# Attention probabilities of four head pairs turned by DMA transposes, in a two-layer hybrid attention trunk

## The chip, the cores and the metric

The kernel runs on one core of a Trainium2 chip. The metric is device time in microseconds (us) of one execution, the median of several runs. One execution was also recorded by the hardware profiler; all rows of the profile come from that one.

The engines of a core have the names of the profile: PE is TensorE (matrix products, with PEld its weight loads), DVE is VectorE, ACT is ScalarE, POOL is GpSimd, SP is SyncE, which does nothing here but issue transfers. Each engine works through its own queue in order. Transfers (DMAs) are issued from a queue of SP, ACT or POOL and run on 16 DMA engines that all queues share. SBUF is the on-chip memory, PSUM the accumulators of TensorE.

## The reference

There are two layers (DEPTH = 2), with 256 tokens of width 2048, all in float32. In each layer two groups of eight heads read the same stream: group A is attention over 64 keys per query that an indexer selects, group B is causal latent attention. Then come an output projection, a layer norm, a SwiGLU feed-forward of width 5632, and another layer norm.

```python
def _hybrid_mixer(x, positions, w_in, g_cq, g_ckv, w_uq, w_ukv, w_o):
    proj = jnp.einsum('bsd,de->bse', x, w_in)
    qa, ka, va, qi, wi, ki, cq, ckv, kr = jnp.split(proj, offsets, axis=-1)
    qa = _rope(...); ka = _rope(...); qi = _rope(...); ki = _rope(...)
    out_a = _dsa_attention(qa, ka, va, qi, ki, wi)
    ...
    out_b = _causal_attention(q_mla, k_mla, v_b, (MLA_NOPE + MLA_ROPE) ** -0.5)
    return jnp.einsum('bse,ed->bsd', jnp.concatenate([out_a, out_b], axis=-1), w_o)

# both attentions, per head
p = jax.nn.softmax(jnp.where(valid, logits, -jnp.inf), axis=-1)
out = jnp.einsum('...', p, v)
```

`_rope` turns the first channels of each head by an angle that depends on the position: `x1*cos - x2*sin` and `x2*cos + x1*sin`.

## The kernel before

**Weights and units.** Weights stream from HBM in units of 128 x 1024 float32 (512 KB). SP issues the load of each into one of four raw buffers (`load_raw`, L342). ACT writes its rounded upper part `wh` (L429), DVE the rest `wl` (L430); five pairs of such buffers exist (`UNITS`). TensorE then runs three products per tile of tokens and slice of the inner dimension: activations' high part by `wh` and by `wl`, and their low part by `wh` (L393 to L395). A unit is 12 such matmuls of 512 columns. A raw buffer is free again when the split has read it, a split buffer when TensorE has.

**Ticks.** Everything that is not a weight product runs as generators (`spawn`, `tick`, `step`, L297 on). After each unit `tick()` is called, and a generator that has said `yield n` goes on n units later. So the order in which the program is traced interleaves one piece of attention with each unit of weights. A scheduler then sets the order of each engine's queue at compile time from that order and its own estimate of when operands are ready; at run time every queue is followed in order. `tc.issue_after(latest["high"])` places an ACT instruction behind the newest `wh`.

**Order of one layer's attention part.** Projection blocks QI0, TA, QI1, TB, KA0 (each 8 units) and the query part of group B; `mla_half(0)`; QA0, VA0; `mla_half(1)`; KA1, QA1, VA1; then `w_o` in 24 units. There are eight pairs of heads per layer. Pairs 0 and 1 of group B run during QA0 and VA0; pairs 0 and 1 of group A (`dsa_attend`) from `mla_half(1)` on; pairs 2 and 3 of group B (`mla_attend`) during QA1; pairs 2 and 3 of group A during `w_o`. Beside them `presums` has POOL load, and DVE add up, weights for the feed-forward.

**One pair** (`attend`, L565). Logits of two heads come into PSUM; DVE scales and masks them into `lg`, one buffer for each tile of 128 queries (128 x 2 x 128 and 128 x 2 x 256, since the first tile sees only 128 keys). `softmax_head` makes probabilities. Some units later TensorE turns them, three 128x128 transposes per head (L583, recorded at L426), ACT copies the three out of PSUM into `pr` (L585), and after another unit TensorE multiplies: V's first block by 256 columns (L592), V's second block by 128 (L593). The profile counts two instructions for each float32 matmul. The result goes to `oT` in two parts.

**Head blocks** (`heads_T`, L608). A finished block of q or k goes through `rope`: DVE writes the two products `ra` and `rb` and adds them into `hd`. With `soon`, TensorE turns the result. Without it (QA0, KA1 and QA1) a DMA transpose does: ACT separates the upper and the lower 16-bit halves of each float32 word into `pl` (L630), ACT's queue issues a transpose of 16-bit elements back into `hd` (L633), and `LAND` = 5 units later ACT puts the halves together (L639). `hidden_by_dma` does the same for the feed-forward, issued by SP (L1074). `dup_rope` (L644) treats the small shared rows in the same way as `heads_T` does.

**Small buffers.** `t2` hands out 2 KB buffers: four that last for the whole kernel and six more during the attention part. All of `lg`, `pr`, `hd`, `ra`, `rb`, `pl`, `dup` and `rel` come from there, in turn by a count.

Of the kernel before, what the change touches and what calls it, by code (L numbers as in the profile page):

```python
# [24 lines left out]
F32 = mybir.dt.float32  # L25
F32R = mybir.dt.float32r
I32 = mybir.dt.int32
U16 = mybir.dt.uint16
# [5 lines left out]
P = 128  # L34
D = 2048
S = 256
# [28 lines left out]
SOON = 200  # L65
FIRSTD = 2
LAND = 5
BEHIND_D, LANDH = 2, 9
T2, T2MORE = 4, 6
ALLFROM, SETSFROM, EARLY = 3, 4, 0  # L70
# [17 lines left out]
def hybrid_trunk(ctx: ExitStack, tc: tile.TileContext, x, xt_in, pos, w_in, g_cq, g_ckv, w_uq,  # L88
# [35 lines left out]
    def t2(shape, s, dt=F32):  # L124
        if phase["name"] == "att":
            phase["t2"] = phase.get("t2", 0) + 1
            if phase["t2"] * T2MORE % (T2 + T2MORE) < T2MORE:
                return pt(shape, dt, s, "t2", T2MORE)
        return sb.tile(shape, dt, name=nm(s), tag="t2", bufs=T2)
# [17 lines left out]
    def trp():  # L147
        return in_turn("tr", 4, 2)
# [126 lines left out]
            nc.scalar.activation(s[:, :, 1, :], a[:, :, lo:hi], AF.Sin)  # L275
            nc.vector.tensor_scalar(s[:, :, 0, :], s[:, :, 1, :], -1.0, None, ALU.mult)

    def rope(dst, src, nh, hd, rot, cos, sin):

        half = rot // 2  # L280
        s3 = src.rearrange("p (h d) -> p h d", d=hd)
        d3 = dst.rearrange("p (h d) -> p h d", d=hd)
        a = t2([P, nh, 2, half], "ra")
        b = t2([P, nh, 2, half], "rb")
        for j in range(2):
            nc.vector.tensor_tensor(a[:, :, j, :], s3[:, :, j * half:(j + 1) * half],
                                    cos.unsqueeze(1).to_broadcast([P, nh, half]), op=ALU.mult)
            nc.vector.tensor_tensor(b[:, :, j, :], s3[:, :, (1 - j) * half:(2 - j) * half],
                                    sin[:, j, :].unsqueeze(1).to_broadcast([P, nh, half]), op=ALU.mult)
        nc.vector.tensor_tensor(d3[:, :, 0:rot], a.rearrange("p h j k -> p h (j k)"),  # L290
                                b.rearrange("p h j k -> p h (j k)"), op=ALU.add)
# [270 lines left out]
        nc.vector.reciprocal(rc, sm)  # L562
        nc.vector.tensor_scalar(lg, lg, rc, None, ALU.mult)

    def attend(logits_of, scale, bias, v_of, oh, ol, h0, wait=3):  # L565


        lgs = []
        lp = att()
        logits_of(h0, [[lp[:, j, 0:P], lp[:, j, P:3 * P]] for j in range(2)])  # L570
        for t in range(NT):
            n = P * (t + 1)
            lg = t2([P, 2, n], "lg")
            nc.vector.scalar_tensor_tensor(lg, lp[:, :, t * P:t * P + n], scale,
                                           bias[t].unsqueeze(1).to_broadcast([P, 2, n]), op0=ALU.mult, op1=ALU.add)
            for j in range(2):
                softmax_head(lg[:, j, :], t, n)
            lgs.append(lg)
        yield wait
        prs = []  # L580
        for j in range(2):
            tp = trp()
            transpose4([lgs[0][:, j, :], lgs[1][:, j, 0:P], lgs[1][:, j, P:]], tp)  # L583
            pr = t2([P, 3 * P], "pr")
            nc.scalar.activation(pr, tp[:, :3 * P], AF.Copy)  # L585
            prs.append(pr)
        yield 1
        op = trp()
        for j, pr in enumerate(prs):
            v0, v1 = v_of(h0 + j)  # L590
            ov = op[:, j * S:(j + 1) * S]
            mm(ov, v0, pr[:, 0:S], start=True, stop=False)  # L592
            mm(ov[:, P:], v1, pr[:, S:], start=False, stop=True)  # L593
        split(oh.rearrange("p j t -> p (j t)"), ol.rearrange("p j t -> p (j t)"), op)


    def layer(l, xT, norms, last):
# [10 lines left out]
        def heads_T(o, nh, hd, rot, cos, sin, dst, soon=False):  # L608


            ss = []
            for t in range(NT):
                s = t2([P, C], "hd")
                if rot < hd:
                    nc.scalar.activation(s, o[t], AF.Copy)
                rope(s, o[t], nh, hd, rot, cos[t], sin[t])
                ss.append(s)
            if soon:
                yield 3
# [7 lines left out]
            for s in ss:  # L627
                h16 = t2([P, 2 * C], "pl", U16)
                with tc.issue_after(latest["high"]):
                    nc.scalar.activation(h16.rearrange("p (h c) -> p h c", h=2),  # L630
                                         s.bitcast(U16).rearrange("p (c h) -> p h c", h=2), AF.Copy)
                v = s.bitcast(U16).rearrange("p (k t) -> p k t", t=P)
                nc.scalar.dma_start_transpose(v, h16)  # L633
                turned.append(v)
                yield 1
            yield LAND
# [6 lines left out]

        def dup_rope(src, cos, sin, rot):  # L644

            s = t2([P, 2, 64], "dup")
            nc.scalar.activation(s[:, 0, :], src, AF.Copy)
            rope(s[:, 0, :], src, 1, 64, rot, cos, sin)
            nc.vector.tensor_copy(s[:, 1, :], s[:, 0, :])
            return s  # L650

# [133 lines left out]
        def mla_attend(hp, m, wait, *before):  # L785
# [7 lines left out]
            def logits(h0, dst):  # L793
# [7 lines left out]
                for t in range(NT):  # L801
                    for j in range(2):
# [3 lines left out]
            h0 = 2 * hp  # L806
            yield from attend(logits, M_SCALE, [causal(masks["c"], t) for t in range(NT)],
                              lambda h: (vb[:, 0, (h % 4) * P:(h % 4 + 1) * P], vb[:, 1, (h % 4) * P:(h % 4 + 1) * P]),
                              oT["B"][0][:, h0:h0 + 2, :], oT["B"][1][:, h0:h0 + 2, :], h0, 3 if hp else 4)

        def dsa_qk(b, soon=False):
            dst = t4([P, 4, S], F32, "qk")
# [11 lines left out]
        def dsa_attend(hp, kaT, qaT, va, wait, *before):  # L824
# [6 lines left out]
            def logits(h0, dst):  # L831
                for j in range(2):
                    for t in range(NT):
# [4 lines left out]
            h0 = 2 * hp  # L838
            yield from attend(logits, A_SCALE, bias,
                              lambda h: (va[:, 0, (h % 4) * P:(h % 4 + 1) * P], va[:, 1, (h % 4) * P:(h % 4 + 1) * P]),  # L840
                              oT["A"][0][:, h0:h0 + 2, :], oT["A"][1][:, h0:h0 + 2, :], h0)

        ready = {}

# [515 lines left out]
```

## Time and profile before

| what | value |
|---|---|
| median of 3 runs | 2127.56 us (2126.53 to 2128.63) |
| the profiled execution | 2126.52 us |
| its span, first to last instruction | 2124.7 us |
| mean granted TensorE clock | 0.998 |
| instructions | 28238 |
| HBM read, written | 503.89 MB, 31.46 MB |

The attention part of the first layer, from QA0 to the end of `w_o`, lies at about 140 to 360 us of the span, that of the second at about 1200 to 1415 us; the feed-forward takes most of the rest. The profile puts lengths of matmuls that overlap one beside the other: the distance between the starts of two neighbours is what one of them costs. A "share" of DMA is the mean busy share of the 16 engines; it can pass 1.00 when packets overlap.

### The profile page before, as it was taken

The numbers are of one execution on the slowest core, as the hardware profiler recorded it, in microseconds if no ns is written. First come the engines' busy times: TensorE is split into PE (matmuls) and PEld (weight loads), VectorE is DVE, ScalarE is ACT, GpSimd is POOL, SyncE is SP. The second block draws the span as 40 slices with busy tenths as digits, with TensorE's granted clock in tenths as the row PEclk, the third lists the DMA queues.
The fourth block names the chain that finished last, engine by engine and source line by source line (L and its number), as shares of the span: only waits on it lengthen the run. The fifth ranks groups of instructions, "written<-read, shape, count | busy, mean of one in ns | idle before, by whom it ended". The sixth has DMA issues, their size and how long they took to land.

```text
span 2124.7 us, 28238 instructions
## 1 busy us (share of the span) xinstructions
PE 2110.9 (99%) x9768; PEld 1748.6 (82%) x9768; DVE 1841.4 (87%) x2324; ACT 1397.2 (66%) x1767; POOL 331.0 (16%) x527
## 2 busy tenths in 40 slices
PE   9999999999999999999999999999999999999998
PEld 8888888888888888888888888888887888888886
DVE  7696776899999999999767976778999999999996
ACT  6556654766777777777555566547667777777773
POOL 1222220020111111011112232201201111111111
PEclk9999999999999999999999999999999999999999
DMA  8688889589899999998757888885999999999994
GB/s 310 206 298 296 307 292 322 182 226 287 232 281 288 279 281 303 292 277 269 225 175 243 300 292 292 324 281 188 240 272 259 288 304 280 283 283 295 303 304 135
DMA packets 213887, 573.40 MB, mean 270 GB/s; under 512 B 68992, under 2 KB 69296, under 8 KB 213104
## 3 DMA queue, kind: packets, MB, share of 16 engines
q1 hardware_dynamic: 149184, 409.39, 55.9%
q0 software_dynamic: 51600, 158.67, 28.9%
q10 hardware_dynamic: 12960, 3.54, 1.1%
q8 instruction: 76, 1.25, 0.2%
q14 instruction: 67, 0.55, 0.1%
HBM read 503.89 MB, written 31.46 MB: 252 GB/s over the span
## 4 chain that ended last, share of the span: by engine, by line
PE 80%; DVE 12%; issue 5%; ACT 2%; DMA 1%; POOL 0%; DVEq 0%; ACTq 0%; POOLq 0%
PE acc L393 9%; PE acc L394 9%; PE acc L395 9%; PE acc L1222 7%; PE acc L1223 7%; PE acc L1221 7%; DVE wl L430 6%; PE gu_p L1106 5%; PE gu_p L1107 4%; PE gu_p L1104 4%; PE gu_c L1107 3%; PE gu_c L1106 3%; PE gu_c L1104 3%; ACT wh L429 2%; PE att L1107 1%
## 5 line engine op out<-in xcount | busy, mean ns | idle before, releaser
L430 DVE TENSOR_TENSOR wl<-raw,wh 128x1024 fp32r<-128x1024 f32 (+2 forms) x919 | 1083.9, 1212 | 202.0 <-ACT wh L429 199.5
L429 ACT ACTIVATE wh<-raw 128x1024 fp32r<-128x1024 f32 (+2 forms) x919 | 936.7, 1048 | 455.4 <-PE acc L395 121.3
L393 PE MATMUL acc<-wh,xhl 128*128 128x512 f32 (+1 forms) x756 | 297.0, 393 | 0.0
L395 PE MATMUL acc<-wh,xhl 128*128 128x512 f32 (+1 forms) x756 | 292.1, 387 | 0.0
L394 PE MATMUL acc<-wl,xhl 128*128 128x512 f32 (+1 forms) x756 | 291.6, 386 | 0.0
L1222 PE MATMUL acc<-wl,hT 128*128 128x512 f32 x640 | 249.3, 390 | 0.2
L1223 PE MATMUL acc<-wh,hT 128*128 128x512 f32 x640 | 249.1, 389 | 0.0
L1221 PE MATMUL acc<-wh,hT 128*128 128x512 f32 x640 | 247.2, 390 | 0.0
L393 PEld LDWEIGHTS acc<-wh,xhl 128*128 128x128 f32 x756 | 142.0, 188 | 30.2 <-issue 3.6
L395 PEld LDWEIGHTS acc<-wh,xhl 128*128 128x128 f32 x756 | 141.9, 188 | 27.3
L394 PEld LDWEIGHTS acc<-wl,xhl 128*128 128x128 f32 x756 | 142.1, 188 | 26.4 <-DVE wl L430 1.1
L1230 POOL DMA_DIRECT2D x<-d x88 | 75.7, 879 | 425.4 <-ACT d L1229 424.2
L1222 PEld LDWEIGHTS acc<-wl,hT 128*128 128x128 f32 x640 | 120.1, 188 | 26.5 <-DVE wl L430 1.4
L1221 PEld LDWEIGHTS acc<-wh,hT 128*128 128x128 f32 x640 | 120.1, 188 | 25.0
L1223 PEld LDWEIGHTS acc<-wh,hT 128*128 128x128 f32 x640 | 120.2, 188 | 24.8
L1106 PE MATMUL gu_c<-wl,xhl 128*128 128x512 f32 x348 | 136.1, 391 | 0.0
L1104 PE MATMUL gu_c<-wh,xhl 128*128 128x512 f32 x348 | 135.5, 389 | 0.3 <-ACT wh L429 0.3
L1107 PE MATMUL gu_c<-wh,xhl 128*128 128x512 f32 x348 | 135.5, 389 | 0.0
L1229 ACT ACTIVATE d<-acc 128x512 f32<-128x512 f32 x88 | 52.1, 595 | 72.9 <-PE acc L1223 69.5
L1106 PE MATMUL gu_p<-wl,many 128*128 128x512 f32 x240 | 94.2, 393 | 0.7 <-DVE wl L430 0.2
L1107 PE MATMUL gu_p<-wh,many 128*128 128x512 f32 x240 | 93.5, 389 | 0.0
L1104 PE MATMUL gu_p<-wh,many 128*128 128x512 f32 x240 | 93.3, 390 | 0.0
(313 smaller groups left out, 3871.9 us busy)
## 6 DMA issues: line engine op xcount, KB each, us to landing
raw<-in_w_gate_dram SPq DMA_DIRECT2D x176, 512.0 KB, 5.8
raw<-in_w_down_dram SPq DMA_DIRECT2D x176, 512.0 KB, 7.6
raw<-in_w_in_dram SPq DMA_DIRECT2D x144, 512.0 KB, 5.7
sum<-in_w_up_dram POOLq DMA_DIRECT2D x118, 512.0 KB, 7.8
raw<-in_w_up_dram SPq DMA_DIRECT2D x103, 512.0 KB, 6.1
raw<-in_w_o_dram SPq DMA_DIRECT2D x64, 512.0 KB, 6.2
q<-q POOLq DMA_DIRECT2D x56, 512.0 KB, 5.2
raw<-q SPq DMA_DIRECT2D x56, 512.0 KB, 7.0
```

Of the source, the lines that this page charges most:

```text
L393: mm(o[t][:, :n], h, a, start=first, stop=False)
L394: mm(o[t][:, :n], h, b, start=False, stop=False)
L395: mm(o[t][:, :n], l, a, start=False, stop=final)
L429: high = nc.scalar.activation(hi, src, AF.Copy)
L430: nc.vector.tensor_tensor(lo, src, f(hi), op=ALU.subtract)
L1104: mm(o[name], h, a, start=name not in begun, stop=False)
L1106: mm(o[name], h, b, start=False, stop=False)
L1107: mm(o[name], l, a, start=False, stop=end)
L1221: mm(o[c][t], h, wh[:, j, :], start=begin, stop=False)
L1222: mm(o[c][t], h, wl[:, j, :], start=False, stop=False)
L1223: mm(o[c][t], lo, wh[:, j, :], start=False, stop=end)
L1230: nc.gpsimd.dma_start(xt[t][:, c * C:(c + 1) * C], d, accum_op=ALU.add)
```

## The change

Three things are changed.

1. `attend` gets `by_dma`, set for the pairs 2 and 3 of group B and 0 and 1 of group A, in both layers. Such a pair is turned the way head blocks are: one unit after the softmax, ACT separates the halves of the first tile's probabilities into a plane buffer of 512 16-bit columns, and a unit later SP issues the transpose back into `lg`; the second tile (1024 columns) follows by one unit. `PLAND` = 4 units later ACT puts the halves together, now into the plane buffer, one tile per unit; after another unit TensorE multiplies. Because the two tiles' turned probabilities now lie in two buffers, V's first block is multiplied by 128 columns twice.
2. The transposes of the head blocks are issued by SP in place of ACT.
3. The products of `rope` share one buffer for both tiles of a block, where they fit (group A and the indexer), and in `dup_rope` lie in the buffer of the rows themselves.

```diff
+PLAND = 4
...
-    def rope(dst, src, nh, hd, rot, cos, sin):
+    def rope(dst, src, nh, hd, rot, cos, sin, room=None):
...
-        a = t2([P, nh, 2, half], "ra")
-        b = t2([P, nh, 2, half], "rb")
+        a, b = room or (t2([P, nh, 2, half], "ra"), t2([P, nh, 2, half], "rb"))
...
-    def attend(logits_of, scale, bias, v_of, oh, ol, h0, wait=3):
+    def attend(logits_of, scale, bias, v_of, oh, ol, h0, wait=3, by_dma=False):
...
+        if by_dma:
+            yield 1
+            planes, turned = [], []
+            for t, lg in enumerate(lgs):
+                n = P * (t + 1)
+                h16 = t2([P, 4 * n], "pl", U16)
+                flat = lg.rearrange("p j n -> p (j n)").bitcast(U16)
+                with tc.issue_after(latest["high"]):
+                    nc.scalar.activation(h16.rearrange("p (h n) -> p h n", h=2), flat.rearrange("p (n h) -> p h n", h=2), AF.Copy)
+                yield 1
+                v = flat.rearrange("p (k t) -> p k t", t=P)
+                nc.sync.dma_start_transpose(v, h16)
+                planes.append(h16)
+                turned.append(v.rearrange("p (h k) t -> p h k t", h=2))
+            yield PLAND
+            for h16, v in zip(planes, turned):
+                with tc.issue_after(latest["high"]):
+                    nc.scalar.activation(h16.rearrange("p (k t h) -> p h k t", h=2, t=P), v, AF.Copy)
+                yield 1
+            first, second = (h16.bitcast(F32).rearrange("p (j b t) -> p j b t", j=2, t=P) for h16 in planes)
+            prs = [((first[:, j, 0], second[:, j, 0]), second[:, j, 1]) for j in range(2)]
+        else:
...
         op = trp()
-        for j, pr in enumerate(prs):
+        for j, (ahead, behind_) in enumerate(prs):
...
-            mm(ov, v0, pr[:, 0:S], start=True, stop=False)
-            mm(ov[:, P:], v1, pr[:, S:], start=False, stop=True)
+            n = S // len(ahead)
+            for i, v in enumerate(ahead):
+                mm(ov[:, i * n:(i + 1) * n], v0, v, start=i == 0, stop=False)
+            mm(ov[:, P:], v1, behind_, start=False, stop=True)
...
+            rooms = [None] * NT
+            if 2 * NT * nh * rot <= C:
+                both = t2([P, NT, 2, nh, 2, rot // 2], "rab")
+                rooms = [(both[:, t, 0], both[:, t, 1]) for t in range(NT)]
...
-                rope(s, o[t], nh, hd, rot, cos[t], sin[t])
+                rope(s, o[t], nh, hd, rot, cos[t], sin[t], rooms[t])
...
-                nc.scalar.dma_start_transpose(v, h16)
+                nc.sync.dma_start_transpose(v, h16)
...
-            s = t2([P, 2, 64], "dup")
+            s = t2([P, 4, 64], "dup")
             nc.scalar.activation(s[:, 0, :], src, AF.Copy)
-            rope(s[:, 0, :], src, 1, 64, rot, cos, sin)
+            rope(s[:, 0, :], src, 1, 64, rot, cos, sin,
+                 [s[:, 2 + i, :rot].rearrange("p (n j k) -> p n j k", n=1, j=2) for i in range(2)])
+            s = s[:, 0:2, :]
...
-                              oT["B"][0][:, h0:h0 + 2, :], oT["B"][1][:, h0:h0 + 2, :], h0, 3 if hp else 4)
+                              oT["B"][0][:, h0:h0 + 2, :], oT["B"][1][:, h0:h0 + 2, :], h0, 3 if hp else 4, hp >= 2)
...
-                              oT["A"][0][:, h0:h0 + 2, :], oT["A"][1][:, h0:h0 + 2, :], h0)
+                              oT["A"][0][:, h0:h0 + 2, :], oT["A"][1][:, h0:h0 + 2, :], h0, by_dma=hp < 2)
```

More of the change, by code (lines that the diff above doesn't have):

```diff
@@ L578, in attend @@
             lgs.append(lg)
[L579 to L587, printed above, removed]
+        if by_dma:
[20 more added lines that the diff above has]
+        else:
+            yield wait
+            prs = []
+            for j in range(2):
+                tp = trp()
+                transpose4([lgs[0][:, j, :], lgs[1][:, j, 0:P], lgs[1][:, j, P:]], tp)
+                pr = t2([P, 3 * P], "pr")
+                nc.scalar.activation(pr, tp[:, :3 * P], AF.Copy)
+                prs.append(((pr[:, 0:S],), pr[:, S:]))
+            yield 1
```

## The prediction

> **What bounds the kernel now.** I read the page first, for the shares of the engines.
>
> ```profile
> PE 2110.9 (99%) x9768; PEld 1748.6 (82%) x9768; DVE 1841.4 (87%) x2324; ACT 1397.2 (66%) x1767; POOL 331.0 (16%) x527
> ```
>
> TensorE is busy for 2110.9 of 2124.7 us, so 13.8 us are idle in the whole span. Then the view of who waited for whom, for TensorE alone, whole run. Columns: who waited for whom, us in total, times, longest.
>
> ```profile
> PE acc L201 <- POOL ident masks.py:199: 1.6, 1, 1.6
> PE gu_p L1106 <- DVE wl L430: 0.4, 2, 0.2
> PE gu_c L1104 <- ACT wh L429: 0.3, 1, 0.3
> PE tr L592 <- ACT pr L585: 0.2, 1, 0.2
> ```
>
> These are 2.5 us, and one of the waits (0.2 us) stands in the code that changes. Third, the busy time by stretch. Columns: stretch, its length, busy PE, PEld, DVE, ACT, POOL, granted clock, DMA share, GB/s. The pairs that change lie in the first and the last row.
>
> ```profile
> 200.00:265.00 65.00, 65.00 (x334) 54.39 (x334) 50.13 (x106) 41.63 (x77) 18.56 (x26) 1.00 0.85 291
> ...
> 285.00:295.00 10.00, 10.00 (x48) 8.35 (x47) 4.37 (x4) 6.88 (x8) 1.04 (x3) 1.00 1.03 417
> 380.00:1020.00 640.00, 639.44 (x2829) 526.22 (x2828) 606.99 (x594) 467.07 (x526) 82.22 (x108) 1.00 0.90 269
> 1260.00:1320.00 60.00, 60.00 (x298) 49.42 (x297) 46.47 (x102) 36.56 (x70) 17.27 (x25) 1.00 0.89 306
> ```
>
> TensorE has no gap in either stretch and its clock is full. So a change there is worth what it takes off TensorE's own sequence, less the stalls that it brings. It cannot be worth more by curing waits: there are none to cure.
>
> **The change, part by part.** *Term 1, the transposes that go.* Each of the four pairs per layer loses two groups of three 128x128 transposes (L583, issued at L426), eight pairs in all, 48 transposes. The order of TensorE's instructions around one such group of six, with columns start, length, line:
>
> ```profile
> 158.97 0.39 PE L395 MATMUL acc<-wh,xhl 128*128 128x512 f32 x1
> 159.20 0.81 PE L426 MATMUL tr<-ident,lg 128*128 128x128 f32 x6
> 159.77 0.47 PE L393 MATMUL acc<-wh,xhl 128*128 128x512 f32 x1
> 160.09 0.39 PE L394 MATMUL acc<-wl,xhl 128*128 128x512 f32 x1
> ```
>
> The lengths overlap, so the price is in the starts. Weight matmuls start 0.23 us apart (158.97 to 159.20). From the first transpose to the second matmul after them is 0.89 us; less the one matmul in it, six transposes cost 0.89 - 0.23 = 0.66 us, 0.11 us each. 8 x 0.66 = 5.3 us, and I take 5.2, since some groups lie against other short matmuls and save the change of kind.
>
> The duration of one transpose is another number:
>
> ```profile
> L426 PE MATMUL tr<-ident,lg x96: 270/272/329, 159.2 to 1368.1; 128*128 128x128 f32 x96
> ```
>
> If each took its 0.272 us alone, 48 would be 13.1 us. The starts say otherwise: six of them occupy 0.66 us, not 1.63. [...]
>
> *Term 2, the product with V that is split.* Each of the 16 heads now multiplies V's first block with two separate 128-column halves instead of one piece of 256 (L592). The rows of one pair's product:
>
> ```profile
> 163.46 0.38 PE L593 MATMUL tr<-pr,vb 128*128 128x128 f32 x2
> 163.68 0.60 PE L592 MATMUL tr<-pr,vb 128*128 128x256 f32 x2
> 164.11 0.38 PE L593 MATMUL tr<-pr,vb 128*128 128x128 f32 x2
> ```
>
> A matmul of 128 columns (two instructions) takes 163.68 - 163.46 = 0.22 us, one of 256 takes 164.11 - 163.68 = 0.43. Two halves are 0.44, 0.01 more: 0.2 us for 16 heads. What is new is a run of six 128-column instructions with a weight load ahead of each, which no row shows. The nearest rows with a load ahead of every instruction are these, of 256 columns in the faster type:
>
> ```profile
> 195.03 0.28 PE L766 MATMUL acc<-cqT,wh 128*128 128x256 f32 x1
> 195.15 0.28 PE L767 MATMUL acc<-cqT,wl 128*128 128x256 f32 x1
> ```
>
> They start 0.12 us apart. At that pace six instructions are 0.72 instead of 0.65, 1.1 us for 16 heads. Nothing makes them shorter, so the bounds are 0 and 1.1; I take 0.2, from the rows of the same instruction.
>
> *Term 3, ScalarE.* Rows of the copies: two of probabilities out of PSUM (L585) go from each pair; a plane copy (L630's kind) and a copy back (L639's kind) come for each of two tiles, of which the first is half as long.
>
> ```profile
> L585 ACT ACTIVATE pr<-tr x32: 463/476/491, 162.4 to 1368.4; 128x384 f32<-128x384 f32 x32
> ...
> L630 ACT ACTIVATE pl<-hd x12: 1040/1054/1059, 172.9 to 1321.9; 128x1024 uint16<-128x1024 uint16 x12
> ...
> L639 ACT ACTIVATE qk<-hd x12: 1354/1357/1368, 197.4 to 1343.0; 128x1024 uint16<-128x1024 uint16 x12
> ```
>
> Out go 0.95 us a pair; in come about 1.5 x (1.05 + 1.36) = 3.6. That is +2.7 us a pair, 11 us a layer on ScalarE, which has 23 us free in the 65 us of the first stretch. Against it, the twelve issues of the head blocks (L633) leave ScalarE's queue:
>
> ```profile
> L633 ACTq DMA_TRANSPOSE hd<-pl x12: 1248/1345/2743, 174.0 to 1323.0; - x12
> ...
> DMA to landing us min/median/max: 3.1/4.8/7.4
> ```
>
> 12 x 1.35 = 16 us of ScalarE's time. Neither reaches TensorE while weights are prepared ahead. How far ahead they are, in 140 to 290 us, is in the waits of ScalarE:
>
> ```profile
> ACT wh L429 <- PE acc L395: 24.6, 17, 2.2
> ...
> ACT wh L429 <- DMA raw<-in_w_in_dram: 5.3, 4, 1.9
> ```
>
> Seventeen times a split waited for TensorE to give a buffer back, four times for a transfer. There are five split buffers, a unit is 12 matmuls of 0.227 us = 2.72 us, so at those moments four units, 10.9 us, were ready. That is the cover of terms 3 and 4; if it is gone, each us of delay costs one.
>
> *Term 4, SP's queue and the transfers.* SP gets 28 transposes: 12 moved and 16 new. Each waits for its plane copy on ScalarE, and behind it stand the weight loads of later units (L342). The rows of the transposes that SP issues today in the FFN, SP's wait ahead of them, and what SP does in 140 to 290 us:
>
> ```profile
> L1074 SPq DMA_TRANSPOSE g<-e x36: 1231/1638/4322, 478.8 to 2008.8; - x36
> ...
> DMA to landing us min/median/max: 3.5/4.9/15.5
> ```
>
> ```profile
> SPq L1074 <- ACT wh L429: 27.4, 16, 2.1
> ```
>
> ```profile
> SPq L342 <- DVE wl L430: 123.9, 43, 7.4
> ```
>
> SP idles 123.9 of those 150 us for want of a free raw buffer, so 12 issues of 1.3 to 1.6 us find room. A pair of issues holds the loads behind it for 3 us, with the longest wait and a long issue twice, 2 x (2.1 + 2.74) = 9.7 us; both are under 10.9. Each copy back follows its transpose by five units, 13.6 us, against 4.9 to landing. The queue of ScalarE shows what a transfer takes:
>
> ```profile
> q10 hardware_dynamic: 12960, 3.54, 1.1%
> ```
>
> 1.1% of 2124.7 us is 23.4 us of all 16 engines, nearly all for twelve transposes: 1.9 us each. A new pair is 1.5 such: 12 in all, 11.5 us a layer. In 200 to 265 us the share is 0.85, and 1.03 is reached elsewhere (285 to 295): 0.18 x 65 = 11.7 us free. It just fits. [...]
>
> *Term 5, buffers.* Sharing the rope products takes three buffers less per head block of the narrow rotations and four less per two duplicated rows; same instructions, no time. A pair now holds four of the ten t2 buffers for about eight units. When QA1's heads come, KA1's two and two pairs' eight fill all ten, so its products wait up to two units, 5.4 us, also under the cover.
>
> Sum: -5.2 + 0.2 = **-5.0 us**, bounds -5.3 (5.3 and 0) and -4.1 (5.2 and 1.1) before stalls. The profiled execution took 2126.52 us (span 2124.7); the median shown is 2127.56, so **2122.5**.
>
> **Rivals.** *A, given back.* Loads late behind transposes, or a weight stream that sets its own pace later. In 290 to 380 us there is a place where the cover is thin:
>
> ```profile
> ACT wh L429 <- DMA raw<-in_w_o_dram: 12.0, 7, 5.7
> ```
>
> There the split waits for transfers. If TensorE comes 2.5 us earlier per layer and the weights do not, 2 x 2.5 us is spent waiting: 2127.5, and in part, 2124 to 2127. Against it: loads are issued as buffers come free, so they move with TensorE, and no stall on weights stands there today.
>
> *B, slower.* SP's order: the 9.7 us hold comes while the transfers are already behind, so the cover was not rebuilt since the group before (six groups in some 80 us). One group per layer fully exposed costs 2 x 9.7 = 19.4: 2141.9. It decides against the change from 5.0 us of exposed hold on, and makes it measurably slower from 9.3. For it: the crowding of term 4. Against: SP's usual wait is 27.4/16 = 1.7 us, and the free time.
>
> *C, by durations.* Transposes worth their 0.272 us each: 2127.56 - 13.1 + 0.2 = 2114.7. The starts speak against it. [...]
>
> That transposes leave TensorE's sequence without shortening it would need idle time there; the stretches show none.
>
> **How the numbers follow.** Forecast 0.47, A 0.35, B 0.13, C 0.05. About 0.2% (4.25 us) is what a measurement of this kernel can tell from no change, so the forecast is only just beyond it: faster 0.47 + 0.05 = 0.52, same 0.35, slower 0.13. The range goes from 2119.5 (the forecast with the upper bound of term 1 and the spread of the runs, 2 us) up over A into the small end of B, 2131.0; that leaves out C and most of B, under 2 in 10.
>
> **What would show it.** Right: 48 rows of transposes from the probabilities instead of 96; 0.66 us a pair between the same two weight matmuls gone; product with V within 0.1 us of today's; busy PE near 2106 and its waits still some 3 us. Wrong: waits of TensorE on L429/L430 in 200 to 300 or 1260 to 1360 us (A, B); long SP waits on the plane copies, landings over 13 us and splits waiting for them (B); six 128-column instructions spaced over 0.12 us (term 2).

## The result, and the profile after

The changed kernel takes 2140.96 us (median of 6 runs, 2135.45 to 2147.48), the kernel before 2128.1 us (6 runs). The ratio is 1.0059, with a 95% interval of 1.0049 to 1.0069: 0.6% slower, where a gain of 0.24% was forecast and 2131.0 us was the end of the range. The profiled execution of the changed kernel took 2141.45 us, its span is 2139.7 us.

First the page of the changed kernel, busy time of each engine:

```profile
PE 2113.2 (99%) x9752; PEld 1748.2 (82%) x9752; DVE 1839.5 (86%) x2324; ACT 1415.9 (66%) x1783; POOL 327.3 (15%) x527
```

Sixteen instructions have left TensorE on balance, and yet it is busy 2.3 us longer and idle for 26.5 us of the span instead of 13.8. Who TensorE waited for, whole run, the changed kernel (us, times, longest):

```profile
PE att L865 <- DVE lg L574: 4.5, 2, 2.8
PE acc L393 <- ACT wh L429: 4.4, 2, 2.3
...
PE acc L1251 <- DVE e L1176: 1.5, 2, 1.2
PE acc L394 <- DVE wl L430: 1.4, 2, 0.8
PE gu_p L1136 <- DVE wl L430: 1.2, 2, 1.0
```

Before, TensorE waited for no split in the attention. Now it does, and the places are the stretches in which the pairs were changed, and what follows them (columns: stretch, length, PE, PEld, DVE, ACT, POOL, clock, DMA share, GB/s):

```profile
200.00:265.00 65.00, 62.15 (x305) 51.00 (x304) 44.76 (x93) 43.65 (x76) 16.62 (x26) 1.00 0.91 280
1260.00:1320.00 60.00, 59.99 (x295) 49.43 (x294) 41.51 (x85) 37.86 (x65) 14.02 (x24) 1.00 0.95 290
1320.00:1345.00 25.00, 22.03 (x95) 17.86 (x95) 18.16 (x32) 18.19 (x26) 5.34 (x8) 0.86 0.84 257
```

All rows of TensorE's waits, those left out here too, add up to 15.1 us; before, they add up to 2.5. The difference, 12.6 us, is most of the 15.0 us by which the two spans differ. The rest is busy time: TensorE is busy longer although work has left. In e11 below, which gives it the same instructions, it is busy for 2106.8 us, 6.4 less.

The largest single stall of the first layer is the one at 260 us. TensorE's timeline of the changed kernel (start, length, line):

```profile
260.15 0.39 PE L395 MATMUL acc<-wh,xhl 128*128 128x512 f32 x1
262.63 0.50 PE L393 MATMUL acc<-wh,xhl 128*128 128x512 f32 x1 [2.09 <-ACT wh L429]
263.89 0.51 PE L394 MATMUL acc<-wl,xhl 128*128 128x512 f32 x1 [0.76 <-DVE wl L430]
...
265.36 0.63 PE L393 MATMUL acc<-wh,xhl 128*128 128x512 f32 x1
265.78 0.63 PE L394 MATMUL acc<-wl,xhl 128*128 128x512 f32 x1
```

It stands still for want of the next unit's `wh` and then its `wl`. Why they are late is in ScalarE's timeline just before, of the same kernel:

```profile
245.90 1.63 ACT L587 ACTIVATE pl<-lg 128x512 uint16<-128x512 uint16 x2
247.44 0.58 ACT L429 ACTIVATE oA<-tr 128x512 fp32r<-128x512 f32 x1
247.92 1.05 ACT L429 ACTIVATE wh<-raw 128x1024 fp32r<-128x1024 f32 x1
252.98 0.78 ACT L596 ACTIVATE pl<-lg 128x512 uint16<-128x512 uint16 x1 [4.01 <-DMA lg<-pl]
253.63 1.03 ACT L429 ACTIVATE wh<-raw 128x1024 fp32r<-128x1024 f32 x1
254.57 1.35 ACT L667 ACTIVATE qk<-hd 128x1024 uint16<-128x1024 uint16 x1
258.04 1.37 ACT L596 ACTIVATE pl<-lg 128x1024 uint16<-128x1024 uint16 x1 [2.12 <-DMA lg<-pl]
...
261.53 1.04 ACT L429 ACTIVATE wh<-raw 128x1024 fp32r<-128x1024 f32 x1
```

Read the gaps in brackets. ScalarE stands at L596, the copy back of a pair's turned probabilities, for 4.01 and again for 2.12 us, until the transfer has landed. The weights' splits (L429) are behind it in the same queue. From 247.92 to 261.53 us it splits two units, and TensorE uses one in 2.72 us, five in that time. The whole run has these waits thirteen times in sixteen copies (the row of ScalarE's waits, changed kernel, then the same view for 140 to 290 us alone):

```profile
ACT pl L596 <- DMA lg<-pl: 29.5, 13, 6.0
```

```profile
ACT pl L596 <- DMA lg<-pl: 13.9, 6, 4.0
...
ACT wh L429 <- PE acc L395: 11.5, 8, 2.2
```

In the second fence the splits wait 8 times for TensorE to give a buffer back; before it was 17 times. That wait is the sign of a full supply of weights, and it has become rare.

VectorE is held up by the same: it comes to the next pair's logits (L574) late because `wh` is late, and it finds the small buffer for them free. Neither VectorE nor ScalarE waits for a small buffer that a transpose still uses anywhere in this trace. VectorE's timeline of the changed kernel:

```profile
254.70 1.23 DVE L430 TENSOR_TENSOR wl<-raw,wh 128x1024 fp32r<-128x1024 f32 x1 [4.47 <-ACT wh L429]
255.84 1.01 DVE L574 SCALAR_TENSOR_TENSOR lg<-att,cmask 128x256 f32<-128x256 f32 x2
```

The two stalls at L865, 4.5 us, come some 40 us later in each layer. There VectorE stands behind splits whose weights land late: in 265 to 302 us ScalarE waits 10.6 us for loads of `w_o`, and in the same stretch before it did not wait for one. Why these loads are late was not traced.

### The profile page after: what moved, and what is told of

It reads as the page before. It is cut to its first block, busy times and chain, and to the rows that moved or that the text cites. A ratio compares the mean times of both kernels' runs of the same rounds, so it can differ in the third digit from the quotient of the medians.

```text
span 2139.7 us, 28271 instructions
## 1 busy us (share of the span) xinstructions
PE 2113.2 (99%) x9752; PEld 1748.2 (82%) x9752; DVE 1839.5 (86%) x2324; ACT 1415.9 (66%) x1783; POOL 327.3 (15%) x527
## 4 chain that ended last, share of the span: by engine, by line
PE 73%; DVE 10%; DMA 7%; issue 6%; ACT 4%; POOL 0%; SPq 0%; ACTq 0%; DVEq 0%; POOLq 0%
PE acc L393 8%; PE acc L394 8%; PE acc L395 8%; PE acc L1252 6%; PE acc L1253 6%; PE acc L1251 6%; DVE wl L430 5%; PE gu_p L1136 4%; PE gu_p L1137 4%; PE gu_p L1134 4%; PE gu_c L1137 2%; ACT wh L429 2%; PE gu_c L1136 2%; PE gu_c L1134 2%; DMA lg<-pl 2%
## 5 line engine op out<-in xcount | busy, mean ns | idle before, releaser
L429 ACT ACTIVATE wh<-raw 128x1024 fp32r<-128x1024 f32 (+2 forms) x919 | 936.6, 1048 | 439.6 <-PE acc L395 111.0
L350 POOL DMA_DIRECT2D sum<-in_w_up_dram x59 | 50.0, 847 | 294.9 <-DMA sum<-in_w_up_dram 293.1
L1137 PE MATMUL gu_p<-wh,many 128*128 128x512 f32 x240 | 93.5, 389 | 0.0
```

The lines of the kernel that those rows point to most:

```text
L429: high = nc.scalar.activation(hi, src, AF.Copy)
L1137: mm(o[name], l, a, start=False, stop=end)
```

## The experiments

Four theories were set up from this. **S**: ScalarE waits in its queue for the landings of the pairs' transposes. **Q**: SP, waiting for a softmax or a plane copy ahead of a transpose, holds the weight loads behind it. **D**: sixteen more transposes are too much for the DMA engines. **B**: the small buffers (`t2`) are held until transposes land, and VectorE waits for one. Two more came up on the way: **SB**, S and B together, each enough by itself, and **O**, the mere lateness of a pair's end in every queue. Ratios are to the kernel before.

**e1, the rest of the change alone.** No pair by DMA; the head blocks' transposes on SP and the shared rope products stay.

```diff
-                              ..., h0, 3 if hp else 4, hp >= 2)
+                              ..., h0, 3 if hp else 4)
...
-                              ..., h0, by_dma=hp < 2)
+                              ..., h0)
```

> Parts 2 and 3 of the change alone: head blocks' transposes in SP's queue, rope products shared, and all pairs turned by TensorE as before. Work of TensorE as before. Theory S (ScalarE waits in its queue for transposes of the pairs to land): no pair is turned by DMA, so nothing is lost: 2127 to 2129 us, ratio 0.999 to 1.001. Theory Q (SP's transposes hold up the weight loads behind them): the 12 head transposes still hold SP, some 23 of the 67 us of such waits in the changed kernel, so about a third of the stalls: 2131 to 2134, ratio 1.002 to 1.003. Theory D (more transfers crowd the DMA engines): as many transfers as before, 1.000.

2126.64 us, 0.9994 (0.9985 to 1.0003). The whole loss comes from the pairs. e1 is the base for the kernels below that add something.

**e2, copies back that do not read the transposes.** It leaves the turned probabilities out: the copies back read `ident`.

```diff
-  nc.scalar.activation(h16.rearrange("p (k t h) -> p h k t", h=2, t=P), v, AF.Copy)
+  nc.scalar.activation(h16.rearrange("p (k t h) -> p h k t", h=2, t=P),
+                       ident.bitcast(U16)[:, None, None, 0:P].to_broadcast([P, 2, v.shape[2], P]), AF.Copy)
```

> The changed kernel, with the copies back of the pairs reading a constant tile in place of the turned probabilities: this leaves the turned probabilities out of the product with V. Same instructions, same transfers, same place in every queue; only the wait of these copies for the landing is gone. Theory S: the 29.5 us that ScalarE waits at L596 are gone and most of the 18 us of stalls with them: 2123 to 2127 us, ratio 0.9975 to 0.9995. Theories Q and D: the transposes stand where they stood in SP's queue and move as many bytes: 2137 to 2142, ratio 1.004 to 1.006.

2140.66 us, 1.0055 (1.0038 to 1.0073), and it tells nothing about S. The wait was still there, 27.9 us in 11 copies, since the copy writes the plane buffer that the transpose is still reading.

**e3, all attention transposes from ScalarE's queue.**

```diff
-                nc.sync.dma_start_transpose(v, h16)
+                nc.scalar.dma_start_transpose(v, h16)
```

> The changed kernel with all transposes of the attention part issued from ScalarE's queue, none from SP's. Theory Q: SP never stands before a transpose there, weight loads go out as buffers come free: 2124 to 2130 us, ratio 0.998 to 1.001 (28 issues of 1.3 us go to ScalarE). Theory S: ScalarE still waits for the landings, and issues on top: 2138 to 2146, ratio 1.005 to 1.009. Theory D: 2138 to 2142.

2169.39 us, 1.0189 (1.0174 to 1.0205). This is longer than any of the theories had it. ScalarE now issues as well and still waits 34.1 us in 10 copies for landings; TensorE waits for `wh` 9.7 us. SP is not the engine that is short of time here.

**e4, copies back four units later.**

```diff
-PLAND = 4
+PLAND = 8
```

> The changed kernel with PLAND = 8 in place of 4: the copies back are traced four units later. Theory S: ScalarE comes to the copies some 11 us later, when all transposes (2.4 to 9.3 us to landing) are there; the waits at L596 fall from 29.5 to under 5 us: 2122 to 2128 us, ratio 0.997 to 1.000. Theories Q and D: transposes and loads go out as before: 2137 to 2142, ratio 1.004 to 1.006; and buffers are held longer, which can only cost.

2142.94 us, 1.0074 (1.0048 to 1.0099). ScalarE's waits for landings at L596 are gone and nothing is gained: S alone does not give the time. But the edit does two things, since later copies back also hold the pair's planes longer. In place of the waits at L596 VectorE waits 7.9 us once, at the first instruction of a pair (L574), for a transpose of a head block that still uses the small buffer it is to write, and ScalarE waits 3.9 us in three plane copies (L587) for the same reason.

**e5, sixteen unused transposes on SP** on top of e1, from V into `cq`.

```diff
...
+            if middle:
+                yield 1
+                for c, n in zip(middle[0], (512, 1024)):
+                    yield 1
+                    nc.sync.dma_start_transpose(c.bitcast(U16)[:, :n].rearrange("p (k t) -> p k t", t=P),
+                                                middle[1][:, 0, :].bitcast(U16)[:, :n])
...
```

> The kernel of e1 (pairs turned by TensorE) with the sixteen transposes of the pairs added as a load alone: at the same two units after the softmax SP issues a transpose of 512 and one of 1024 columns, out of the values of V (ready long before) into a buffer that nothing reads any more. No engine waits for them and SP waits for nothing before them. Theory D (the DMA engines are crowded, so weights and transposes land later): 2132 to 2139 us, ratio 1.002 to 1.005. Theory Q (SP is held up by its waits before the transposes) and theory B (small buffers are held until the transposes land, and VectorE waits in its queue for one): 2126 to 2129, ratio 0.999 to 1.001.

2137.7 us, 1.0044 (1.0027 to 1.0062). Not a clean test of D: two pairs wrote the same tile, so SP itself waited for the earlier transposes to land and issued no weight load for 14 us; ScalarE waits 10.83 us for one unit of weights, up to 228.75 us.

**e6, SP held at the same points, with next to no bytes:** e1 and a transfer of 8 words per partition out of each logits buffer, where the transposes stood.

```diff
...
+                for i in range(2):
+                    yield 1
+                    nc.sync.dma_start(dsrc[:, 8 * i:8 * i + 8], lgs[i][:, 1, 0:8])
...
```

> The kernel of e1 with, at the same two units, a tiny transfer (8 words per partition) of the pair's probabilities issued by SP: SP waits there for the softmax as it does for the plane copies in the changed kernel, and the weight loads behind wait with it; next to no bytes are moved and nobody waits for them. Theory Q: 2132 to 2139 us, ratio 1.002 to 1.005. Theories D and B: 2126 to 2130, ratio 0.999 to 1.001.

2125.92 us, 0.9988 (0.9978 to 0.9997). SP did wait for the softmax there:

```profile
SPq L606 <- DVE lg L564: 16.9, 8, 4.9
```

Eight holds of up to 4.9 us cost nothing. That speaks against Q, which was the slower rival of the prediction. But the changed kernel holds SP longer, 44.0 us in 15 waits of up to 7.9 us ahead of the pairs' transposes (L590). What clears Q is e11 below: 50.0 us in 16 such waits of up to 8.8 us, and no loss.

**e7, the larger plane of a pair in `cq`** (the compressed queries, not read any more by then), not in a small buffer.

```diff
-                h16 = t2([P, 4 * n], "pl", U16)
+                h16 = spare.bitcast(U16) if t else t2([P, 4 * n], "pl", U16)
...
-                              ..., h0, 3 if hp else 4, hp >= 2)
+                              ..., h0, 3 if hp else 4, hp >= 2, cq[hp % 2])
...
-                              ..., h0, by_dma=hp < 2)
+                              ..., h0, by_dma=hp < 2, spare=cq[hp % 2])
```

> The changed kernel with the second tile's planes of each pair in the two buffers of the compressed queries, which are not read any more by then, in place of two of the ten small ones: a pair holds three small buffers in place of four. Transfers and queues as in the changed kernel. Theory B: VectorE's waits for a small buffer go, 2126 to 2134 us, ratio 0.999 to 1.003. Theories D and Q: 2137 to 2143, ratio 1.004 to 1.007.

2142.5 us, 1.006 (1.0036 to 1.0084). B alone falls. ScalarE's waits for landings remain:

```profile
ACT pl L596 <- DMA lg<-pl: 22.4, 6, 7.8
...
ACT cq L596 <- DMA lg<-cq: 16.4, 7, 5.1
```

**e8, only pairs 0 and 1 of group A by DMA.**

```diff
-                              ..., h0, 3 if hp else 4, hp >= 2)
+                              ..., h0, 3 if hp else 4)
```

> The changed kernel with only group A's pairs 0 and 1 turned by DMA (four pairs in all in place of eight). 2.5 us less work for TensorE. If the loss comes pair by pair (theory Q), half of the stalls stay: 2132 to 2135 us, ratio 1.002 to 1.0035. If it comes only where transposes of pairs and of head blocks crowd together in QA1 and VA1 (theories D and B), nearly none stay: 2124 to 2129, ratio 0.998 to 1.0005.

2139.8 us, 1.0047 (1.003 to 1.0064): half the pairs, most of the loss (more than either range had it), and by another stall. TensorE's waits in e8:

```profile
PE tr L426 <- DVE oA L430: 5.8, 2, 2.9
```

Group B's pair 2 turns on TensorE again, and its transposes wait for `oA`, the split of the product of group A's pair 1, which now ends just ahead of them. Both use the few PSUM pieces that `trp` hands out. That gave O.

**e9, e5 with other places:** the extra transposes read the pair's own logits and write `kiT` and `cq`.

```diff
...
+                for c, lg in zip(middle, lgs):
+                    yield 1
+                    u = lg.rearrange("p j n -> p (j n)").bitcast(U16)
+                    nc.sync.dma_start_transpose(c.bitcast(U16).rearrange("p (k t) -> p k t", t=P), u)
...
-                              ..., h0, 3 if hp else 4, hp >= 2)
+                              ..., h0, 3 if hp else 4, middle=(kiT, cq[hp % 2]) if hp >= 2 else None)
...
-                              ..., h0, by_dma=hp < 2)
+                              ..., h0, middle=(kiT, cq[hp % 2]) if hp < 2 else None)
```

> The changed kernel with its turned probabilities taken out again (rope rooms and the head transposes on SP stay: e1, 2126.6 us), plus two unused DMA transposes for each of the middle pairs: they read the pair's logits one unit after its softmax, of the changed kernel's size and on the same queue, and write two tiles that nobody reads afterwards (kiT, cq). TensorE's own transposes and the order of all other work stay as in e1. D (the DMA engines are too full for 16 more transposes): 2136 to 2143 us. O (the pair's end comes some five units later in every queue, and that is what costs): 2126 to 2129. SB (each of two waits is enough by itself: ScalarE's for the landing, VectorE's for a buffer held until the landing): 2126 to 2130, since nothing waits for these landings.

2138.97 us, 1.0047 (1.0032 to 1.0062). That is D's number, but see e11 and e15. At one place ScalarE waits 10.76 us for one unit of weights (SP's timeline, then ScalarE's, e9):

```profile
1309.81 1.83 SPq L342 DMA_DIRECT2D raw<-in_w_in_dram  x3
...
1317.29 11.67 SPq L606 DMA_TRANSPOSE cq<-lg  x1
```

```profile
1326.17 1.06 ACT L429 ACTIVATE wh<-raw 128x1024 fp32r<-128x1024 f32 x1 [10.76 <-DMA raw<-in_w_in_dram]
```

The load that it waits for was the first of the three at 1309.81 us, so it took over 16 us to land. Then SP waits 2.9 us for the previous pair's transpose into `kiT`, and one issue takes 11.67 us, in which no load goes out.

**e10, late without DMA:** e1 with the middle pairs' TensorE transposes 8 units after the softmax and not 3.

```diff
-                              ..., h0, 3 if hp else 4)
+                              ..., h0, 8 if hp >= 2 else 3 if hp else 4)
...
-                              ..., h0)
+                              ..., h0, 8 if hp < 2 else 3)
```

> e1 (2126.6 us) with the middle pairs' TensorE transposes moved from 3 units after the softmax to 8, so that the product with V and the split come as late in the order as in the changed kernel, with no DMA transpose and no plane copy. O: 2135 to 2143 us. D: 2126 to 2128. SB: 2126 to 2130 (the logits' buffers are held five units longer, but for no landing).

2129.1 us, 1.0006 (0.9997 to 1.0016). O costs 2.5 us against e1 when all four pairs of a layer are late together.

**e11, both waits taken away:** e7 with PLAND 7. (Its label says 8; it is 7, since with 8 the plane of a later pair would overwrite `cq` too soon.)

```diff
-PLAND = 4
+PLAND = 7
...
-                h16 = t2([P, 4 * n], "pl", U16)
+                h16 = spare.bitcast(U16) if t else t2([P, 4 * n], "pl", U16)
...
```

> The changed kernel with PLAND at 7 (with 8 alone ScalarE's waits for landings were gone, 2142.9 us) and the larger plane of each pair in cq and not in the small buffers (alone 2142.5 us): both waits taken away at once. SB: 2120 to 2127 us. D: 2138 to 2144. O: 2138 to 2146.

2125.59 us, 0.9985 (0.9974 to 0.9996), with the same sixteen transposes at the same places. All waits of ScalarE and VectorE for a pair's landings or a held buffer are gone, and the stretches are whole again:

```profile
200.00:265.00 65.00, 65.00 (x323) 54.08 (x322) 48.42 (x104) 46.97 (x81) 16.43 (x26) 1.00 0.98 298
1260.00:1320.00 60.00, 60.00 (x291) 49.55 (x290) 44.22 (x100) 44.12 (x75) 14.62 (x24) 1.00 1.04 302
```

The engines moved more here (298 GB/s at a share of 0.98) than in the changed kernel (280 at 0.91). So they were not what held it: D falls as the cause of its loss. e11 is faster than both kernels, by 0.15% than the one before.

**e12, the head blocks back on TensorE,** so that as many bytes of transposes leave as the pairs add.

```diff
-        def dsa_qk(b, soon=False):
+        def dsa_qk(b, soon=True):
```

> The changed kernel with the three head blocks of each layer that went through DMA transposes (QA0, KA1, QA1) turned by TensorE instead: as many bytes of DMA transposes leave (6 of 128x512 a layer) as the pairs' 8 add, and TensorE gets its 48 transposes back, about 5 us. D: 2124 to 2130 us, the crowding being gone. O: 2136 to 2143. SB: 2132 to 2143, the pairs' waits being still there.

2146.97 us, 1.0085 (1.0067 to 1.0104). Fewer bytes and a longer time, longer than any of the theories had it. TensorE's transposes of the heads meet the split of a late pair, as in e8:

```profile
PE tr L426 <- DVE oA L430: 11.6, 2, 7.0
```

**e13, e11 with the planes in the small buffers again** (PLAND 7 and nothing else).

```diff
-PLAND = 4
+PLAND = 7
```

> The changed kernel with PLAND 7 and nothing else: it differs from e11 (2125.6 us) only in that the larger plane of a pair lies in the small buffers again. SB: 2135 to 2144 us, with hardly a wait of ScalarE for landings and a wait of VectorE for a small buffer held by a transpose in the attention. If it was the distance of 7 units (and not 8, as in e4) that helped e11, with no part of the buffers in it: 2123 to 2128.

2134.44 us, 1.003 (1.002 to 1.0041), just below the range of SB. ScalarE waits for no landing at L596. But VectorE and ScalarE now wait for a small buffer, ScalarE ahead of a pair's plane copy (the waits of each in e13, then VectorE's timeline):

```profile
DVE lg L574 <- DMA hd<-pl: 8.1, 2, 4.3
```

```profile
ACT pl L587 <- DMA hd<-pl: 6.4, 2, 4.5
```

```profile
253.62 1.23 DVE L430 TENSOR_TENSOR wl<-raw,wh 128x1024 fp32r<-128x1024 f32 x1 [0.55 <-ACT wh L429]
258.58 1.02 DVE L574 SCALAR_TENSOR_TENSOR lg<-att,cmask 128x256 f32<-128x256 f32 x2 [3.73 <-DMA hd<-pl]
```

The buffer that the count hands out for `lg` is one that a head block's transpose still uses. TensorE stops at 260 us as in the changed kernel, for another reason. This is B, shown by itself: 8.9 us between e13 and e11.

**e14, e11 with PLAND 5.**

```diff
-PLAND = 7
+PLAND = 5
```

> e11 with PLAND 5 and not 7, the larger planes in cq: how many units the copy back must stand behind the transpose. SB with a threshold near the landings of 9 to 11 us: ScalarE's waits for landings are about half of e7's (PLAND 4, 2142.5 us) and the time lies between, 2128 to 2139 us. If one more unit is enough: 2124 to 2128.

2128.53 us, 1.0002 (0.999 to 1.0013). One unit more than in e7 takes away most of the waits (e14):

```profile
ACT pl L596 <- DMA lg<-pl: 10.0, 6, 3.6
...
ACT cq L596 <- DMA lg<-cq: 2.2, 3, 1.3
```

12.2 us are left of e7's 38.8, and TensorE has no stall in 200 to 290 or 1260 to 1340 us that comes from them. The cover takes a third of such waits, not all.

**e15, eight extra transposes from V** on top of e1, the larger size only, no destination used twice in a row. **e16, the same from the pair's logits.**

```diff
...
+                c, vt = middle
+                nc.sync.dma_start_transpose(c.bitcast(U16).rearrange("p (k t) -> p k t", t=P), vt[:, 0, :].bitcast(U16))
...
# e16 in place of it
+                nc.sync.dma_start_transpose(c.bitcast(U16).rearrange("p (k t) -> p k t", t=P),
+                                            lgs[1].rearrange("p j n -> p (j n)").bitcast(U16))
```

> e1 (2126.6 us) with one unused transpose for each middle pair, of the larger size (128x1024 two-byte elements): it reads V, which stays where it is for long, and writes cq, each pair another one than the pair before, so that neither SP nor any buffer waits for a landing. Two thirds of the bytes of e9 (2139.0 us). D: 2133 to 2138 us. Without D: 2126 to 2129.

> e15 with the pair's own logits as the source, after the softmax: the same bytes and queue, but the small buffer of the logits is held until the transpose has landed, and SP waits for the softmax. If the held buffer is what cost e9 its time: 2131 to 2138 us where e15 stays at 2126 to 2129. D: like e15, 2133 to 2138. Neither: 2126 to 2129 in both, and what cost e9 time is that two transposes stand together and the second pair's wait on SP for the first pair's to land in kiT.

e15: 2127.05 us, 0.9994 (0.9985 to 1.0003). e16: 2137.88 us, 1.0042 (1.0029 to 1.0056). From issue to landing, e15 and then e16:

```profile
DMA to landing us min/median/max: 5.8/7.5/9.3
```

```profile
DMA to landing us min/median/max: 4.0/13.1/15.9
```

By the numbers this is the held buffer, but the trace of e16 does not bear that out: neither VectorE nor ScalarE waits in it for a landing of these transposes; the splits wait for late weights (45.9 us for `w_in` against e15's 13.5). Nor are the two alike in time: with V ready early, SP issued e15's transposes at 192 to 206 us, e16's at 209 to 257. Why transposes took 13 us there and at most 11.0 in e11 stays open. So extra transposes can cost time by themselves, in e9 and e16, and the runs do not show how. It is not needed for the changed kernel, in which no transpose of a pair took over 9.3 us.

**e17, e11 with pairs 0 and 1 of group A only; e18, with pairs 2 and 3 of group B only.**

```diff
# e17, against e11
-                              ..., h0, 3 if hp else 4, hp >= 2, cq[hp % 2])
+                              ..., h0, 3 if hp else 4)
# e18, against e11
-                              ..., h0, by_dma=hp < 2, spare=cq[hp % 2])
+                              ..., h0)
```

> e11 (PLAND 7, larger planes in cq) with only the pairs 0 and 1 of group A through DMA transposes; pairs 2 and 3 of group B turn on TensorE again: 24 transposes gone instead of 48, 2.6 us of TensorE instead of 5.2 against e1 (2126.6 us), and half the transposes' bytes. If what e11 leaves (4 of its 5.2 us) goes to the weights that arrive later behind 16 transposes, half of the transposes leave less of it: 2123.5 to 2125.5 us. If it goes to FFN stages that have no slack whatever arrives earlier: 2125 to 2127. If the late end of these two pairs and the shared PSUM pieces of the next pair's own transposes are what e8 lost its 12 us to: 2130 to 2138.

> The other half: e11 with only the pairs 2 and 3 of group B through DMA transposes. With the weights as the residue: 2123.5 to 2125.5 us; with FFN stages without slack: 2125 to 2127; nothing behind these pairs turns on TensorE before the barrier ahead of the last two pairs of group A, so that e8's stalls are not expected in any case.

e17: 2134.79 us, 1.0028 (1.0015 to 1.004). The stall is e8's, 6.9 us on `oA` in two places, and there is no wait for a pair's landing. So half of the pairs has a loss of its own kind: a pair that ends late against the next pair's own transposes. e18: 2130.82 us, 1.0011 (0.9999 to 1.0022), longer than both of its ranges. It has one stall of 3.6 us at L865 and one of 2.5 us at the start of the feed-forward, so neither half shows the residue of e11 cleanly.

## Why the prediction was wrong, step by step

The four kernels with all pairs by DMA, one beside the other:

| | planes in small buffers | larger planes in `cq` |
|---|---|---|
| PLAND 4 | 1.0059; ScalarE waits 29.5 us for landings | 1.006 (e7); 38.8 us |
| PLAND 7 | 1.003 (e13); VectorE waits 8.1 us, ScalarE 6.4 us for a buffer | 0.9985 (e11); neither |

With the waits of ScalarE in place the buffers make no difference; with them gone the buffers are worth 0.45%. Only both cures together bring the time below that of before. In the changed kernel itself S is what the trace shows; it has no wait for a held buffer. Taking S away by distance alone (e13) brings back 6.5 of the 12.9 us, and B's waits come up in its place. Whether B lay hidden behind S before or came with the longer distance, the runs do not separate. **SB fits all four in this form**, and the waits of e4 too; why one unit more than in e13 costs 8.5 us more in e4 stays open.

- **The step that failed is in term 4**: "Each copy back follows its transpose by five units, 13.6 us, against 4.9 to landing." Five units in the order of the program are not five units of time between the two. SP's timeline of the changed kernel:

```profile
246.65 1.31 SPq L590 DMA_TRANSPOSE lg<-pl  x1
...
248.75 1.96 SPq L590 DMA_TRANSPOSE lg<-pl  x1
```

ScalarE came to the copies back at 252.98 - 4.01 = 248.97 and 258.04 - 2.12 = 255.92 us: 2.3 and 7.2 us behind the issues. ScalarE splits weights up to four units ahead of TensorE, and its queue shows what is left of the distance: one split of a unit of weights (L429, `wh`) stands between the first issue and its copy back, that at 247.92 us, and one between the second and its own, that at 253.63 us, where the program has five units. In all sixteen copies of the changed kernel it is one or two splits, in e11, with three units more, three or four. What remains between is gone through as fast as operands come. The landing, 4.9 us by the feed-forward's rows, was right for the median and not for the longest (changed kernel, L590):

```profile
DMA to landing us min/median/max: 2.4/5.0/9.3
```

- **Term 5 had the mechanism and lost it to the cover.** "so its products wait up to two units, 5.4 us, also under the cover": e13 measured such a wait at up to 4.3 us, at the logits and not the rope products, and it was not covered. In the changed kernel no such wait is seen.
- **The cover of 10.9 us** was counted once for each term. It is one stock, used by ScalarE's waits, the copies and the late loads together, and it is refilled only as fast as ScalarE, VectorE and the loads outrun TensorE. Before, a split waited for TensorE, with the stock full, 17 times in 140 to 290 us (24.6 us in all); in the changed kernel 8 times (11.5 us), in e11 9 times (18.2 us). That the stock is one for all these waits is argued from the rows; no run changes its size.
- **Term 1 and term 2 were right.** 48 rows of transposes from the probabilities are left. The lower price of groups beside other short matmuls comes to 0.01 us a group in the trace of before: from the first of six transposes to the matmul behind them (L835) it is 0.65 us (212.03 to 212.68), against 0.66 beside weight matmuls. And e11, where the pairs' stalls are gone, is busy 2106.8 us on TensorE ("near 2106" was forecast). A pair's product with V in the changed kernel:

```profile
228.36 0.61 PE L616 MATMUL tr<-pl,va 128*128 128x128 f32 x4
228.80 0.39 PE L617 MATMUL tr<-pl,va 128*128 128x128 f32 x2
229.03 0.61 PE L616 MATMUL tr<-pl,va 128*128 128x128 f32 x4
229.47 0.39 PE L617 MATMUL tr<-pl,va 128*128 128x128 f32 x2
```

Six instructions of 128 columns from 228.36 to 229.03: 0.67 us against 0.65 before, 0.3 us for 16 heads, with no extra price for the weight loads.

- **Term 3's work was right**: +2.7 us a pair makes 21.6 us for eight; ScalarE is busy 1415.9 instead of 1397.2 us, 18.7 more. Not the work but the waiting ate the cover.
- **Rival B** gave nearly the time (2141.9 us) by the wrong mechanism, which is luck: e6 held SP eight times for nothing, and e11 sixteen times. **"It just fits"** held: e11 carries all transposes at a share of 0.98 and 1.04 in the two stretches.
- **The range's lower end** does not follow from its own terms: 2122.5 less 0.3 and less 2 is 2120.2, not 2119.5. It changes nothing here.
- **Rival A** is what is left in e11. Of 5 us, about 1 us comes out against e1. TensorE's waits in e11 that e1 has not:

```profile
PE acc L1251 <- DVE e L1176: 1.5, 2, 1.2
PE tr L426 <- ACT wh L429: 1.5, 1, 1.5
PE att L865 <- DVE lg L574: 1.5, 1, 1.5
```

These 4.5 us lie outside the changed stretches, in the second layer's first blocks, in `w_o` and at the start of the feed-forward. That TensorE there runs into weights that come no earlier is argued from these rows; e17 and e18 were to show it and did not. It stays open.

## What to carry to other kernels

Distances in a program's order (so many units between an issue and its use) were worth their time here only on the engine that paces that order: five units are 13.6 us on TensorE, and ScalarE came to the two copies shown 2.3 and 7.2 us behind the issues. On an engine that runs ahead, count what stands between the two in its own queue, and look in its timeline for where it would stand when the transfer lands. A transfer put in place of work on a full engine needs two things checked for each in-order queue it touches: who stands behind the instruction that waits for the landing, and which buffer comes round next while it is in flight; curing one of two such waits can show nothing at all (e4 and e7, 1.0074 and 1.006 beside 1.0059). And take a stock of prepared work as spent once, which is argued above and was not tested: add up all waits that draw on it in one stretch before calling any of them hidden.

## What was not expected of the hardware

The longest stall of the first layer cost TensorE more than its length. The changed kernel's granted clock around the stall at 260 us (the column before the DMA share):

```profile
260.00:265.00 5.00, 2.15 (x9) 1.23 (x8) 2.69 (x8) 5.00 (x11) 1.44 (x2) 0.99 0.50 165
265.00:270.00 5.00, 5.00 (x23) 4.26 (x22) 3.50 (x10) 5.00 (x7) 0.34 (x1) 0.67 1.04 257
270.00:275.00 5.00, 5.00 (x24) 4.11 (x23) 4.17 (x7) 4.54 (x6) 1.22 (x1) 1.00 1.06 251
```

The stall took 2.25 and 1.03 us beyond the usual 0.23 us from start to start, 3.3 us together, with one matmul in between. Some 1 us after it seven matmuls start 0.43 us apart and not 0.23 (265.36 to 265.78 in the timeline above), some 1.4 us more; the granted clock is 0.67 in 265 to 270 us and 1.00 in the next 5 us. The second layer's stall at 1320 us, 2.45 and 1.03 us beyond the usual, has the same behind it: ten matmuls start 0.43 us apart (1324.58 to 1328.85), some 2.0 us more, and the granted clock is 0.80 in 1320 to 1325 us, 0.52 in 1325 to 1330 and 1.00 after. Behind the stall of 1.67 us at L865 in the first layer it stays at 1.00 (300 to 305 us). From what length of a stall on the clock falls was not measured.

A transpose's time to land is not given by its size: 2.4 to 9.3 us in the changed kernel, up to 11.0 in e11, for the same two sizes, and 4.0 to 15.9 in e16 for the larger size alone. What sets it was not measured.
